# Feed-forward and recurrence stages in text order by the generator's clocks, and modulation products beside the down products

## The chip, the cores and the metric

One core of a Trainium2 chip runs the whole program. The metric is the device time of one execution in microseconds (us), the median over several runs. The engines are called as the profile calls them: PE (TensorE), DVE (VectorE), ACT (ScalarE), POOL (GpSimd) and SP (SyncE, which here only issues DMAs).

## The reference

The input is one sequence of 512 tokens of width 1024, all in fp32. Two layers of a modulated block are followed by two layers of a hybrid attention block and a last norm. The change touches the first two layers only. Cut to what matters, they are:

```python
for layer in range(2):
    mod = (silu(c) @ mod_w[layer] + mod_b[layer]).reshape(1, 3, 3, 1024)   # shift, scale, gate
    h, g = sublayer_input(x, norm_g[layer, 0], mod[:, 0])                  # rmsnorm, scale, shift
    x = x + 0.5 * g * swiglu(h, ffn_w_gu[layer, 0], ffn_w_down[layer, 0])
    h, g = sublayer_input(x, norm_g[layer, 1], mod[:, 1])
    y = stick_breaking_attention(h) if layer == 0 else rglru_block(h)
    x = x + g * y
    h, g = sublayer_input(x, norm_g[layer, 2], mod[:, 2])
    x = x + 0.5 * g * swiglu(h, ffn_w_gu[layer, 1], ffn_w_down[layer, 1])

def swiglu(h, w_gu, w_down):                 # w_gu 1024 x 5632, w_down 2816 x 1024
    g, u = split(h @ w_gu, 2)
    return (silu(g) * u) @ w_down

def rglru_block(h, ...):                     # width 1280, 10 blocks of 128
    gate, xb = split(h @ w_in, 2)
    xc = causal_conv(xb)                     # 4 taps
    r, i = sigmoid(xc @ w_r + b_r), sigmoid(xc @ w_i + b_i)
    a = exp(-8 * r * softplus(-lam))
    b = sqrt(-expm1(-16 * r * softplus(-lam))) * (i * xc)
    hs = scan(a, b)                          # hs[t] = a[t] * hs[t-1] + b[t]
    return (gelu(gate) * hs) @ w_out
```

## The kernel before, in words

The token axis is the free axis: `x` lies as eight tiles of 128 channels x 512 tokens. The stages run one after another: ffn00, stick (the attention layer), ffn01, ffn10, lru (the recurrence), ffn11, hybrid layers 0 and 1.

**Products.** An fp32 product is made of three PE matmuls of 512 columns in a reduced format: weight high part by input high part, weight high by input low, weight low by input high. So every operand needs two tiles: for weights `wh` (an ACT cast of the loaded chunk) and `wl` (chunk minus `wh`, on DVE or POOL), for inputs pairs like `hH, hL`, `gH, gL`, `xH, xL`, `yH, yL`, `aH, aL`.

**Stream.** All weights come from HBM in one list of entries (`segments`, L82, `layout`, L197). An entry is a `raw` tile of 128 x 1024 (512 KB), loaded by one DMA on SP's queue into a ring of 4 (`stream_dma`, L581). A weight entry holds 8 slots of 128 x 128, in two halves of 4. Between the weight entries stand 144 modulation entries: a `raw` tile multiplied by `cact` and summed on DVE in one custom instruction (`raw<-raw,cact`), eight of them to a vector such as (0, 2, 1) (layer 0, sublayer 2, scale). The numbers in `mod(0, 2, 1, 0.68, 0.78)` (L99) say between which fractions of its stage's weight stream the eight stand. `stream_step` (L606) converts the next entry; `ahead` keeps four halves converted in front of PE, in rings of five `wh` and five `wl` (L622).

**Normalization.** The first jobs of a stage start on unnormalized input: `begin` (L979) multiplies weights with `gH, gL` (x times its scale) while the column sums of squares (`o<-ones,sq`), the reciprocal root, its spreading by `o<-diag,ones`, and the normalized `ht`, `hH`, `hL` are made. What the shift adds is made apart: `wshift` sums weights times shift on DVE, `T<-ones,wshift` sums it over partitions on PE. At ffn00 that is `start` (L867). `FIRST` (L72) says how many blocks of 128 output columns a feed-forward stage starts in this way.

**Order of work.** One Python generator per little task issues the instructions. A virtual time `vt` goes on with each matmul; `spawn` queues a task, `pump` runs those that are due, and a task's `yield 0.7` comes back 0.7 us of `vt` later. In stick and the hybrid layers the program runs under `planned` (L380): the instructions of PE, DVE, ACT and POOL stand in the engine queues in the order in which the text issues them, each engine has a modelled clock (`clocked`, L390), and a bare `yield` comes back at the modelled end of what the task issued. In ffn00 to ffn11 and lru only the pieces in `begin` and `start` have a fixed order; the rest is ordered by the framework's scheduler.

**Recurrence** (`lru`, L1378). Jobs are `xb0` to `xb9` (then `conv` on DVE, giving `xH, xL`), `ri0` to `ri9` (two small products per block, then `gate_ri`), `ga0` to `ga9` (the gate half of `w_in`), and the output product `wo`. `beta` takes an ACT Sqrt of `om`, then on DVE a product and the scan `om<-ra,ix`. `out` is an ACT Gelu (`ge`) that frees the product's PSUM bank, a DVE product by the scan, and the split into `yH, yL`. There are eight PSUM banks: four `mm`, two `z`, one `T`, one `o`.

Of the kernel before, what the change touches and what calls it, by code (L numbers as in the profile page):

```python
# [71 lines left out]
FIRST = {(0, 0): 6, (0, 1): 4, (1, 0): 4, (1, 1): 4}  # L72
# [9 lines left out]
def segments():  # L82
# [4 lines left out]
    def ffn(l, i, mods):  # L87
# [3 lines left out]
        jobs += [(f"gu{j}", [gu[j]], KD) for j in range(n, 2 * KF)]  # L91
# [3 lines left out]
    def mod(l, s, j, a, b):  # L95
# [3 lines left out]
    ffn(0, 0, [mod(0, 0, 2, 0.16, 0.28), mod(0, 1, 1, 0.28, 0.40), mod(0, 1, 0, 0.40, 0.52), mod(0, 1, 2, 0.52, 0.64),  # L99
               mod(0, 2, 1, 0.68, 0.78), mod(0, 2, 0, 0.78, 0.88), mod(0, 2, 2, 0.88, 0.98)])  # L100
# [36 lines left out]
    jobs += [(f"wo{m}", [wo[m]], KR) for m in range(4, KD)]  # L137
    segs.append(("lru", jobs, []))
# [38 lines left out]
def first_slots(segs):  # L177
# [3 lines left out]
    for name, jobs, _ in segs:  # L181
        for job in jobs:
            for kt in rows_of(job):
                for j, (_, _, cols) in enumerate(job[1]):
# [4 lines left out]
                    slot += len(cols) // 128  # L189
    return out  # L190
# [6 lines left out]
def layout(segs):  # L197

    slots, chunk_span = [], []
    for name, jobs, mods in segs:  # L200
        a = len(slots)
        for job in jobs:
            for kt in rows_of(job):
# [22 lines left out]
    for c in range(len(slots) // 8):  # L226
        if c >= n:
            entries.append(("w", slots[8 * c:8 * c + 8]))
# [115 lines left out]
class Kern:  # L344

    NSLOT = 74

    RAW = 4
    AHEAD = 4

# [10 lines left out]
    def __init__(self, tc, io, upto=None):  # L361
        self.tc, self.nc, self.io = tc, Front(self, tc.nc), io

# [175 lines left out]
    def mm(self, out, lhsT, rhs, start, stop, cost=None):  # L539
# [8 lines left out]
        self.matmul_at(out, (lhsT, rhs), cost, start)  # L548
# [14 lines left out]
    def stream_init(self, entries):  # L563
# [6 lines left out]
        self.w_conv = 0  # L570
        self.n_w, self.kept = 0, []
# [5 lines left out]
        self.act_busy = False  # L577
# [3 lines left out]
    def stream_dma(self):  # L581
        nc = self.nc
        while self.e_dma < len(self.entries):
# [17 lines left out]
            else:  # L601
                break
            self.raws[self.e_dma] = raw
            self.e_dma += 1

    def stream_step(self):  # L606
# [3 lines left out]
        nc = self.nc  # L610
        if e[0] == "mod":
# [5 lines left out]
            if m == KD - 1 and vec != (0, 0, 1):  # L617
                self.mod_end(vec, 0, KD)
        else:
            j = self.w_conv % 2  # L620
            w = raw[j] if type(raw) is list else raw[:, 512 * j:512 * j + 512]
            h = self.wpool.tile([128, 512], F32R, name=self.name("wh"), tag="wh", bufs=self.AHEAD + 1)  # L622
            l = self.wpool.tile([128, 512], F32R, name=self.name("wl"), tag="wl", bufs=self.AHEAD + 1)
            if self.act_busy:
                nc.vector.tensor_copy(h, w)
            else:
                nc.scalar.copy(h, w)
            self.pool_credit += self.pool_low
# [17 lines left out]
        self.stream_dma()  # L646

# [40 lines left out]
    def take(self, n):  # L688
# [3 lines left out]
        self.slot += n  # L692
        h, l = self.parts[c]
# [61 lines left out]
    def mod_of(self, vec):  # L755
        assert (vec, KD - 1) in self.full, vec
# [98 lines left out]
    def h_high(self, kt, gs, shift, bc):  # L855
# [8 lines left out]
        self.h.append((h, l))  # L864
        return lambda: nc.vector.scalar_tensor_tensor(l, t, s, h.bitcast(F32), OP.add, OP.subtract)

    def start(self, tags):  # L867
# [33 lines left out]
        def factors():  # L901
# [27 lines left out]
            self.kept = []  # L929
# [1227 lines left out]
```

## Time and profile before

| | |
|---|---|
| median of 3 runs | 3085.96 us (3082.9 to 3088.1) |
| profiled execution, its own time | 3085.68 us |
| its span in the profile | 3084.0 us |
| mean granted TensorE clock | 0.987 |
| busy: PE, DVE, ACT, POOL | 97%, 62%, 43%, 35% of the span |
| stages: ffn00, stick, ffn01, ffn10 | 0 to 408, 408 to 683, 683 to 1042, 1042 to 1401 us |
| lru, ffn11, hybrid 0, hybrid 1 | 1401 to 1625, 1625 to 1992, 1992 to 2526, 2526 to 3084 us |

Busy is the time that instructions of an engine took, by their records. Matmul records overlap (each is longer than the distance to the next), so PE's busy share does not tell how fast it goes; the distance between starts does. A stage is bounded here by the first matmul of one stage and that of the next. Most helpers record every operation under one line (L328 for DVE, ACT and POOL, L547 for matmuls), so instructions are told apart by their tiles.

### The profile page before, as it was taken

How to read it: one execution, taken by the hardware profiler on the slowest of the kernel's cores; microseconds unless marked ns; L12 is line 12 of the kernel's file. 1: busy time of each engine (PE TensorE's matmuls, PEld its weight loads, DVE VectorE, ACT ScalarE, POOL GpSimd, SP SyncE). 2: the span in 40 equal slices, each digit the busy share in tenths (PEclk: the TensorE clock that was granted, in tenths of full speed). 3: DMA queues.
4: the chain of work that ended last, by engine and by line, in shares of the span. 5: the costliest groups of instructions: out<-in, count | busy, mean ns of one | idle time of the engine just before them, and what ended most of it. 6: DMA issues, size and time to landing. Idle time of an engine off the chain costs nothing. (4 is left out here: it accounts for less than half of the span.)

```text
span 3084.0 us, 39072 instructions
## 1 busy us (share of the span) xinstructions
PE 2977.1 (97%) x13752; PEld 2475.4 (80%) x13752; DVE 1902.0 (62%) x3409; ACT 1312.9 (43%) x2520; POOL 1085.0 (35%) x802
## 2 busy tenths in 40 slices
PE   7999999989999999999899999999999999999998
PEld 5788877768888888887688888888888878888886
DVE  7844476676444655568965333578676556867653
ACT  3333245544332333324734333356456534645652
POOL 4554754440001200013531001343443684334466
PEclk9999999999999999999999999999999999999999
DMA  6454554413333344462222223354343335434322
GB/s 241 158 198 175 194 160 113 119 64 137 137 137 133 120 171 152 156 211 82 81 94 92 96 97 115 110 166 122 103 123 110 109 117 157 123 110 124 110 85 93
DMA packets 132643, 400.53 MB, mean 130 GB/s; under 512 B 18528, under 2 KB 19040, under 8 KB 132448
## 3 DMA queue, kind: packets, MB, share of 16 engines
q1 hardware_dynamic: 132448, 398.04, 39.2%
q8 instruction: 109, 1.79, 0.2%
q14 instruction: 86, 0.70, 0.1%
HBM read 343.44 MB, written 6.30 MB: 113 GB/s over the span
## 5 line engine op out<-in xcount | busy, mean ns | idle before, releaser
L328 POOL TENSOR_TENSOR wl<-raw,wh 128x512 fp32r<-128x512 f32 x574 | 815.3, 1427 | 905.1 <-ACT wh L328 852.2
L328 ACT CAST wh<-raw 128x512 fp32r<-128x512 f32 x968 | 596.0, 620 | 1063.3 <-PE mm L547 926.9
L547 PE MATMUL mm<-hH,wh 128*128 128x512 f32 x1584 | 622.1, 393 | 13.6 <-ACT ge L328 9.8
L547 PE MATMUL mm<-hL,wh 128*128 128x512 f32 x1584 | 620.6, 392 | 2.6 <-DVE hL L328 2.6
L547 PE MATMUL mm<-hH,wl 128*128 128x512 f32 x1584 | 619.7, 391 | 0.0
L328 DVE TENSOR_TENSOR wl<-raw,wh 128x512 fp32r<-128x512 f32 x396 | 290.3, 735 | 363.4 <-ACT wh L328 360.7
L547 PE MATMUL mm<-gH,wh 128*128 128x512 f32 x1016 | 407.2, 401 | 6.2 <-DVE v L328 3.9
L547 PE MATMUL mm<-gH,wl 128*128 128x512 f32 x1016 | 398.5, 392 | 1.5 <-POOL wl L328 1.5
L547 PE MATMUL mm<-gL,wh 128*128 128x512 f32 x1016 | 397.8, 392 | 0.0
L547 PEld LDWEIGHTS mm<-hH,wh 128*128 128x128 f32 x1584 | 299.6, 189 | 77.4 <-ACT ge L328 10.2
L547 PEld LDWEIGHTS mm<-hL,wh 128*128 128x128 f32 x1584 | 299.7, 189 | 67.0 <-DVE hL L328 5.3
L547 PEld LDWEIGHTS mm<-hH,wl 128*128 128x128 f32 x1584 | 299.5, 189 | 62.5
L328 DVE CUSTOM_DVE_ANT_0 raw<-raw,cact 128x1024 f32<-128x1024 f32 x144 | 207.8, 1446 | 187.0 <-DMA raw<-ws 180.1
L547 PE MATMUL mm<-aH,wl 128*128 128x512 f32 x704 | 274.0, 389 | 0.0
L547 PE MATMUL mm<-aH,wh 128*128 128x512 f32 x704 | 273.9, 389 | 0.0
L328 POOL TENSOR_TENSOR sq<-x 128x512 f32<-128x512 f32 x7 | 7.6, 1086 | 730.7 <-DVE x L328 730.7
L547 PEld LDWEIGHTS mm<-gH,wl 128*128 128x128 f32 x1016 | 191.4, 188 | 44.7 <-POOL wl L328 2.7
L547 PEld LDWEIGHTS mm<-gH,wh 128*128 128x128 f32 x1016 | 192.1, 189 | 42.0 <-issue 4.3
L547 PEld LDWEIGHTS mm<-gL,wh 128*128 128x128 f32 x1016 | 192.1, 189 | 35.0
L547 PEld LDWEIGHTS mm<-aH,wl 128*128 128x128 f32 x704 | 132.1, 188 | 27.6 <-POOL wl L328 0.4
L547 PEld LDWEIGHTS mm<-aH,wh 128*128 128x128 f32 x704 | 132.1, 188 | 27.5
L547 PE MATMUL mm<-wide,wh 128*128 128x512 f32 x384 | 149.4, 389 | 0.0
(271 smaller groups left out, 4706.6 us busy)
## 6 DMA issues: line engine op xcount, KB each, us to landing
raw<-ws SPq DMA_DIRECT2D x629, 512.0 KB, 3.3
ks<-rH SPq DMA_DIRECT2D x80, 128.0 KB, 3.2
kl<-rL SPq DMA_DIRECT2D x80, 128.0 KB, 2.6
qs<-rH SPq DMA_DIRECT2D x56, 128.0 KB, 3.9
qs<-rL SPq DMA_DIRECT2D x56, 128.0 KB, 3.7
keep<-ws SPq DMA_DIRECT2D x16, 256.0 KB, 5.9
ks<-qkH SPq DMA_DIRECT2D x32, 128.0 KB, 3.5
kl<-qkL SPq DMA_DIRECT2D x32, 128.0 KB, 3.1
```

The costliest lines, as they stand in the source:

```text
L328: r = f(*args, **kw)
L547: self.nc.tensor.matmul(out, lhsT, rhs, start=start, stop=stop, skip_group_check=True)
```

## The change

It runs ffn01, ffn10, ffn11, lru, and what follows the start of ffn00, under `planned`; fixed waits in the tasks become bare `yield`. In these stages a new mode `free` converts each half chunk (`operand`) and each modulation product (`product_sum`) in a task of its own, and `either` puts each `wl` on POOL or DVE by their modelled clocks. `wh` and `wl` move from rings of five into the common arena (74 to 84 tiles). The modulation vectors of ffn00, ffn01 and ffn10 move to the down products, the last third of a stage, and two of ffn10's six move into ffn01. `FIRST` of ffn01 goes from 4 to 6 blocks. A wait of 6.0 us of `vt` is put ahead of the column sums in `start`, and `begin` waits for the modelled end of `sq`. The table `SEVEN` is empty for every stage, so the code that reads it issues nothing; it is left out below.

```diff
-FIRST = {(0, 0): 6, (0, 1): 4, (1, 0): 4, (1, 1): 4}
+FIRST = {(0, 0): 6, (0, 1): 6, (1, 0): 4, (1, 1): 4}
...
-    ffn(0, 0, [mod(0, 0, 2, 0.16, 0.28), mod(0, 1, 1, 0.28, 0.40), mod(0, 1, 0, 0.40, 0.52), mod(0, 1, 2, 0.52, 0.64),
-               mod(0, 2, 1, 0.68, 0.78), mod(0, 2, 0, 0.78, 0.88), mod(0, 2, 2, 0.88, 0.98)])
+    ffn(0, 0, [mod(0, 0, 2, 0.53, 0.60), mod(0, 1, 1, 0.60, 0.66), mod(0, 1, 0, 0.667, 0.73), mod(0, 1, 2, 0.73, 0.79),
+               mod(0, 2, 1, 0.79, 0.85), mod(0, 2, 0, 0.85, 0.91), mod(0, 2, 2, 0.91, 0.97)])
...
-    ffn(0, 1, [mod(1, 0, 1, 0.05, 0.35), mod(1, 0, 0, 0.35, 0.65), mod(1, 0, 2, 0.65, 0.95)])
-    ffn(1, 0, [mod(1, 1, 1, 0.02, 0.2), mod(1, 1, 0, 0.2, 0.4), mod(1, 1, 2, 0.4, 0.6),
-               mod(1, 2, 1, 0.68, 0.78), mod(1, 2, 0, 0.78, 0.88), mod(1, 2, 2, 0.88, 0.98)])
+    ffn(0, 1, [mod(1, 0, 1, 0.53, 0.65), mod(1, 0, 0, 0.667, 0.74), mod(1, 0, 2, 0.74, 0.81),
+               mod(1, 1, 1, 0.81, 0.88), mod(1, 1, 0, 0.88, 0.96)])
+    ffn(1, 0, [mod(1, 1, 2, 0.667, 0.74), mod(1, 2, 1, 0.74, 0.81), mod(1, 2, 0, 0.81, 0.88), mod(1, 2, 2, 0.88, 0.96)])
...
-    NSLOT = 74
+    NSLOT = 84
...
+    def either(self, out, a, b, op):
+
+        if self.free:
+            t = max(self.made.get(x.tensor.name, 0.0) for x in (a, b))
+            pool = max(self.clock["gpsimd"], t) + 1.29 < max(self.clock["vector"], t) + 0.68 + 0.7
...
+    def product_sum(self, vec, m, raw):
...
+        yield max(0.01, self.made[raw.tensor.name] - self.vt)
+        self.nc.vector.tensor_tensor_reduce(raw, raw, self.cact, 1.0, 0.0, OP.mult, OP.add, accum_out=out[:, m:m + 1])
+        del raw
+        self.in_ring -= 1
+        self.stream_dma()
...
+    def operand(self, i, raws, first):
...
+        self.shifts(w, 4 * i)
+        h = self.t("wh", dt=F32R)
+        self.nc.scalar.copy(h, w)
+        yield
+        l = self.t("wl", dt=F32R)
+        self.either(l, w, h.bitcast(F32), OP.subtract)
...
+            yield 6.0
             late.extend(self.shift_cols((0, 0), 8))
...
         def factors():
-            yield self.CHAIN[0] if (l, s) != (0, 2) else 7.0
+            if self.timed:
+                yield max(0.1, self.made[self.sq[0].tensor.name] - self.vt + 0.1)
...
-                yield 0.7
+                yield
                 nc.vector.tensor_tensor(a, sg, u, OP.mult)
...
+        with self.planned() if not self.timed else contextlib.nullcontext():
+            self.free = True
+            self.ffn_rest(l, i, n, act, low, evac)
+            self.free = False
...
-            yield 3.8
+            yield
             h = self.t("xH", dt=F32R)
...
-        self.pool_low = 1.0
+        self.free = True
         for n in range(4):
             self.spawn(conv(n, ps[n], late[n], tags[n]))
...
-                self.act_busy = n == 2
...
+                with self.planned() if l or i else contextlib.nullcontext():
+                    self.ffn(l, i)
...
+                    with self.planned():
+                        self.lru()
```

In the pieces below a row is one instruction, or several alike (x3), with its line, its operation, its output and inputs (the number behind a name tells tiles apart) and its shape.

DVE behind the start of ffn00, before: `wshift` sums weights times shift, `ISA raw,mod<-raw,cact` is a modulation product, `a` and `wide` belong to the first blocks' activations.

```order
L328 TENSOR_SCALAR wshift_699<-keep_326,mod_365 128x128
L328 ISA raw_740,mod_738<-raw_740,cact 128x1024
L328 ISA mod_738 128x1
L328 SCALAR_TENSOR_TENSOR wshift_699<-keep_326,mod_365,wshift_699 128x128
L328 TENSOR_TENSOR a_835<-sg_834,mm_787 128x512
...
L328 TENSOR_TENSOR wide_83<-a_835,aH_866 128x512
L328 SCALAR_TENSOR_TENSOR wshift_699<-keep_373,mod_365,wshift_699 128x128
L328 ISA raw_789,mod_738<-raw_789,cact 128x1024
L328 ISA mod_738 128x1
L328 SCALAR_TENSOR_TENSOR wshift_699<-keep_373,mod_365,wshift_699 128x128
```

DVE at the same place with the change:

```order
L346 TENSOR_SCALAR wshift_678<-keep_326,mod_365 128x128
L346 SCALAR_TENSOR_TENSOR wshift_678<-keep_326,mod_365,wshift_678 128x128 x3
L346 SCALAR_TENSOR_TENSOR wshift_678<-keep_327,mod_365,wshift_678 128x128 x4
L346 TENSOR_SCALAR wshift_678<-keep_372,mod_365 128x128
L346 SCALAR_TENSOR_TENSOR wshift_678<-keep_372,mod_365,wshift_678 128x128 x3
L346 SCALAR_TENSOR_TENSOR wshift_678<-keep_373,mod_365,wshift_678 128x128 x4
L346 TENSOR_TENSOR a_842<-sg_841,mm_794 128x512
L346 TENSOR_TENSOR wide_83<-a_842,aH_856 128x512
```

The modulation products are gone from among the `wshift` instructions; one pair of `a` and `wide` now stands behind the last of them.

PE at the start of ffn01, before: `mm<-oH/oL` are the last of the attention's output product, `z, mm<-gH/gL` the first of ffn01, `o<-ones,sq` the column sums.

```order
L547 MATMUL mm_5753<-oH_5579,wh_5646 128x512
L547 MATMUL mm_5753<-oL_5581,wh_5646 128x512
L547 MATMUL mm_5753<-oH_5579,wl_5647 128x512
L547 MATMUL z_5788<-gH_5589,wh_5673 128x512
...
L547 MATMUL mm_5790<-gH_5641,wl_5729 128x512
L547 MATMUL o_5842<-ones,sq_5587 128x1 x4
L547 MATMUL mm_5791<-gH_5641,wh_5728 128x512
```

PE at the same place with the change:

```order
L568 MATMUL mm_5760<-oH_5588,wh_5632 128x512
L568 MATMUL mm_5760<-oL_5590,wh_5632 128x512
L568 MATMUL mm_5760<-oH_5588,wl_5654 128x512
L568 MATMUL z_5790<-gH_5598,wh_5684 128x512
...
L568 MATMUL mm_5792<-gH_5598,wl_5718 128x512
L568 MATMUL o_5819<-ones,sq_5596 128x1 x4
L568 MATMUL mm_5793<-gH_5598,wh_5684 128x512
```

The sums stand 33 matmuls behind the last output product before, and 9 behind it now.

ACT in the recurrence, before: `om<-om` is the last Sqrt, `ge` a Gelu that frees a PSUM bank, `yH` the cast behind the product with the scan, `wh` a weight cast.

```order
L328 ACTIVATE om_12158<-om_12158 128x512
L328 ACT_TABLE_LOAD
L328 ACTIVATE ge_12193<-T_12029 128x512
L328 ACTIVATE ge_12195<-o_12116 128x512
L328 CAST wh_12245<-raw_11997 128x512
...
L328 CAST wh_12329<-raw_12121 128x512
L328 CAST yH_12218<-ge_12193 128x512
L328 CAST yH_12220<-ge_12195 128x512
L328 CAST wh_12350<-raw_12202 128x512
L328 ACTIVATE ge_12242<-mm_12197 128x512
L328 CAST yH_12264<-ge_12242 128x512
```

ACT at the same place with the change:

```order
L346 ACTIVATE om_12176<-om_12176 128x512
L346 ACT_TABLE_LOAD
L346 ACTIVATE ge_12227<-T_12063 128x512
L346 ACTIVATE ge_12229<-o_12154 128x512
...
L346 ACTIVATE ge_12268<-mm_12231 128x512
...
L346 ACTIVATE ge_12306<-mm_12270 128x512
L346 CAST wh_12328<-raw_12132 128x512
L346 CAST wh_12330<-raw_12132 128x512
L346 CAST yH_12341<-ge_12227 128x512
L346 CAST yH_12346<-ge_12229 128x512
L346 ACTIVATE ge_12350<-mm_12308 128x512
```

The third, fourth and fifth Gelu stood behind the casts `yH` of the first two blocks; two of them now stand ahead of these casts, the third behind.

## Rows read from the trace of the kernel before

**Rows 1.** The page: busy time, share of the span and instructions of each engine.

```profile
PE 2977.1 (97%) x13752; PEld 2475.4 (80%) x13752; DVE 1902.0 (62%) x3409; ACT 1312.9 (43%) x2520; POOL 1085.0 (35%) x802
```

**Rows 2.** Two stages: length; busy us (count) of PE, PEld, DVE, ACT, POOL; clock, DMA share, GB/s.

```profile
1042.00:1401.00 359.00, 358.83 (x1595) 297.30 (x1595) 209.68 (x332) 117.78 (x194) 30.13 (x21) 1.00 0.48 167
1401.00:1625.00 224.00, 205.19 (x886) 167.06 (x885) 176.53 (x219) 115.36 (x183) 101.89 (x71) 0.95 0.24 83
```

**Rows 3.** Timeline of PE: ffn00's sums and two matmuls behind them; two matmuls of ffn01.

```profile
112.13 0.59 PE L547 MATMUL T<-ones,wshift 128*128 128x1 f32 x2 [5.32 <-DVE wshift L328]
113.58 0.63 PE L547 MATMUL mm<-hH,wl 128*128 128x512 f32 x1
114.00 0.63 PE L547 MATMUL mm<-hH,wh 128*128 128x512 f32 x1
...
676.43 0.39 PE L547 MATMUL z<-gH,wh 128*128 128x512 f32 x1
676.66 0.39 PE L547 MATMUL z<-gL,wh 128*128 128x512 f32 x1
```

**Rows 4.** Waits of PE, 0 to 2000 us: us in total, times, longest us.

```profile
PE mm L547 <- ACT ge L328: 9.8, 1, 9.8
PE T L547 <- DVE wshift L328: 5.3, 1, 5.3
PE o L547 <- DVE sq L328: 5.3, 2, 4.8
PE z L547 <- DVE xL L328: 4.9, 1, 4.9
PE o L547 <- POOL wl L328: 2.3, 1, 2.3
PE mm L547 <- DVE hL L328: 1.7, 3, 0.7
```

**Rows 5.** Short stretches behind two of the waits, columns as in rows 2.

```profile
108.00:118.00 10.00, 5.87 (x16) 4.81 (x17) 7.75 (x20) 2.28 (x5) 3.71 (x2) 0.50 0.54 177
1531.00:1542.00 11.00, 6.15 (x15) 4.86 (x16) 8.90 (x12) 5.51 (x10) 2.55 (x2) 0.53 0.11 43
```

**Rows 6.** Timeline of DVE, 72 to 120 us.

```profile
73.20 1.45 DVE L328 CUSTOM_DVE_ANT_0 raw<-raw,cact 128x1024 f32<-128x1024 f32 x1 [1.03 <-DMA raw<-ws]
...
79.59 1.78 DVE L328 SCALAR_TENSOR_TENSOR hL<-ht,mod,hH 128x512 fp32r<-128x512 f32 x1
...
87.08 0.74 DVE L328 SCALAR_TENSOR_TENSOR hL<-ht,mod,hH 128x512 fp32r<-128x512 f32 x1
...
106.16 1.21 DVE L328 CUSTOM_DVE_ANT_0 raw<-raw,cact 128x1024 f32<-128x1024 f32 x1
...
114.27 0.34 DVE L328 SCALAR_TENSOR_TENSOR wshift<-keep,mod,wshift 128x128 f32<-128x128 f32 x1
```

**Rows 7.** Timeline of ACT, then DVE, in the recurrence.

```profile
1532.45 0.62 ACT L328 CAST yH<-ge 128x512 fp32r<-128x512 f32 x1 [11.32 <-DVE ge L328]
...
1532.34 1.21 DVE L328 TENSOR_TENSOR_SCAN om<-ra,ix 128x512 f32<-128x512 f32 x1
```

**Rows 8.** Timeline of DVE at the end of the attention layer.

```profile
686.26 1.75 DVE L328 TENSOR_TENSOR sq<-sq,sqt 128x512 f32<-128x512 f32 x1
```

**Rows 9.** Stretches with the densest transfers, columns as in rows 2.

```profile
5.00:25.00 20.00, 12.79 (x48) 10.01 (x48) 12.78 (x29) 11.11 (x18) 6.14 (x4) 1.00 1.04 397
280.00:400.00 120.00, 120.00 (x530) 99.06 (x529) 56.06 (x68) 31.39 (x54) 81.38 (x56) 1.00 0.54 193
```

**Rows 10.** The page: a group (count, busy us, mean ns) and the DMA of raw (landing us).

```profile
L328 POOL TENSOR_TENSOR wl<-raw,wh 128x512 fp32r<-128x512 f32 x574 | 815.3, 1427 | 905.1 <-ACT wh L328 852.2
...
raw<-ws SPq DMA_DIRECT2D x629, 512.0 KB, 3.3
```

**Rows 11.** Timeline of POOL, 72 to 92 us.

```profile
77.32 3.50 POOL L328 TENSOR_TENSOR wl<-raw,wh 128x512 fp32r<-128x512 f32 x2 [3.76 <-ACT wh L328]
```

More of the change, by code (lines that the diff above doesn't have):

```diff
@@ L602, in stream_dma @@
                 break
+            for r in raw if type(raw) is list else (raw,):
+                self.made[r.tensor.name] = self.vt + 5.0
             self.raws[self.e_dma] = raw
@@ L610, in stream_step @@
         nc = self.nc
+        if e[0] == "mod" and self.free:
+            self.spawn(self.product_sum(e[1], e[2], raw))
+            del self.raws[self.e_conv]
+            self.e_conv += 1
+            return
         if e[0] == "mod":
@@ new lines, in operand @@
+    def operand(self, i, raws, first):
+        for r in self.reads.setdefault(i, raws):
+            yield max(0.01, self.made[r.tensor.name] - self.vt)
+        w = yield from first()
+        self.shifts(w, 4 * i)
+        h = self.t("wh", dt=F32R)
+        self.nc.scalar.copy(h, w)
+        yield
+        l = self.t("wl", dt=F32R)
+        self.either(l, w, h.bitcast(F32), OP.subtract)
+        self.parts[i] = (h, l)
+        del w, first
+        for r in raws:
+            self.left_raw[r.tensor.name] -= 1
+            if not self.left_raw[r.tensor.name]:
+                self.in_ring -= 1
+                self.stream_dma()
+        self.reads.pop(i)
@@ L692, in take @@
         self.slot += n
+        if c not in self.parts:
+            self.need(lambda: c in self.parts)
         h, l = self.parts[c]
@@ L755, in mod_of @@
     def mod_of(self, vec):
-        assert (vec, KD - 1) in self.full, vec
+        self.need(lambda: all((vec, k) in self.full for k in range(KD)))
         return self.mods[vec]
@@ new lines, in seven, with B, T, product @@
+    def seven(self, f, tt, act, low, last):
+        nc = self.nc
+        def B(k, o):
+            return lambda i: tuple(x[:, o:o + 256] for x in self.h[i + k])
+        def T(k):
+            return lambda i: tuple(x[:, 256 * (i % 2):256 * (i % 2) + 256] for x in tt[k - 1, i // 2])
+        def product(bank, mov, first=True):
+            for i in range(4):
+                xh, xl = mov(i)
+                wh, wl = self.take(1)
+                for n, (w, x) in enumerate(((wh, xh), (wh, xl), (wl, xh))):
+                    self.mm(bank, w, x, first and i == n == 0, i == 3 and n == 2, again=i == n == 0)
+                self.pump()
+        for _ in range(4):
+            self.job(f"q{f}")
+        b1 = self.bank("mm")[:, 0:256]
+        product(b1, B(0, 0))
+        base = self.t("base", 256)
+        nc.scalar.copy(base, b1)
+        b2 = self.bank("z")[:, 0:256]
+        product(b2, T(2))
+        u2 = self.t("u2", 256)
+        nc.vector.tensor_tensor(u2, base, b2, OP.add)
+        self.rel("z")
+        if self.behind:
+            self.behind()
+        b3 = self.bank("z")[:, 0:256]
+        product(b3, T(1))
+        u4 = self.t("u4", 256)
+        nc.vector.tensor_tensor(u4, u2, b3, OP.add)
+        self.rel("z")
+        product(b1, B(4, 0), False)
+        g = self.t("sg")
+        nc.scalar.activation(g[:, 0:256], b1, AF.Silu)
+        self.rel("mm")
+        b7 = self.bank("mm")[:, 0:256]
+        product(b7, T(3))
+        up = self.t("a")
+        nc.vector.tensor_tensor(up[:, 256:512], u4, b7, OP.add)
+        b3 = self.bank("mm")[:, 0:256]
+        product(b3, B(4, 256))
+        nc.vector.tensor_tensor(u4, u4, b3, OP.add)
+        self.rel("mm")
+        def right():
+            yield
+            nc.scalar.activation(g[:, 256:512], u4, AF.Silu)
+        self.spawn(right(), 0.1)
+        def behind():
+            self.behind = None
+            product(b7, T(4), False)
+            nc.vector.tensor_tensor(up[:, 0:256], u2, b7, OP.add)
+            self.rel("mm")
+            self.spawn(rest())
+        def rest():
+            yield 0.1
+            yield
+            nc.vector.tensor_tensor(up, g, up, OP.mult)
+            yield
+            h = self.t("aH", dt=F32R)
+            nc.scalar.copy(h, up)
+            yield
+            lo = low[f] if f < 12 else self.t("aL", dt=F32R)
+            self.either(lo, up, h.bitcast(F32), OP.subtract)
+            act[f] = (h, lo)
+        if last:
+            behind()
+        else:
+            self.behind = behind
```

273 lines of the change are left out of this document (208 added, 65 removed).

## The prediction

> **What bounds the kernel now.** I read the page first: PE is busy 97% of the span [rows 1], so only what stops or slows PE can move the time. Then the stages: ffn10 takes 359 us for 66 weight entries of 24 matmuls, 1584 in all [rows 2], that is 0.227 us from start to start, the distance that two neighbours in ffn01 show too [rows 3]. That stage has nothing to give. The recurrence takes 224 us with PE busy in 205 [rows 2]. The waits of PE say where the idle time up to 2000 us lies [rows 4]: 9.8 us in front of one product of the recurrence, 5.3 in front of ffn00's column sums of `wshift`, 5.3 before sums of squares (4.8 of it at the start of ffn01), 4.9 and 2.3 in the recurrence, 1.7 in three pieces behind `hL`. A wait costs more than itself: after the one that ends at 112.13 us the next matmuls start 0.42 us apart instead of 0.23 [rows 3], with a granted clock of 0.50 against 1.00 in ffn10, and around the end of the 9.8 us the clock is 0.53 [rows 2, 5]. So each matmul in such a stretch loses 0.195 us.
>
> **The change, term by term.** The sum is made against the profiled execution, 3085.68 us (span 3084.0 and 1.7 around it), which lies 0.3 below the median.
>
> *Start of ffn00.* PE stands from 106.8 to 112.1 us, and DVE's last `wshift` starts at 114.27 us and ends about 0.3 later [rows 6]. In front of it in DVE's queue stand four modulation products that now move to the down products: one that waited 1.03 us for its DMA and ran 1.45, and three of 1.21 [rows 6] (two of the three are not shown), together 6.1 us; one pair of `a` and `wide`, two instructions of 0.6 us, moves behind it. So `wshift` would end at 114.6 - 6.1 - 1.2 = 107.3. PE comes to the last of the sums six matmuls (1.4 us) later in its own order, but without the 1.7 us behind `hL`, which two of these products had delayed: 106.8 + 1.4 - 1.7 = 106.5, or up to 3 us later where a block now in text order waits for its `hL`. At most the whole place goes: 5.3 idle, 14 matmuls at 0.195 = 2.7, and 1.7, together 9.7. At least 4.5 goes, where 2.5 us of wait stay and with them the slow stretch. I take 7.5, nearer to the upper end, because `wshift` comes out within 1 us of PE.
>
> *The recurrence.* PE's 9.8 us are a wait for a PSUM bank, which the third block's Gelu frees. That Gelu stood on ACT behind `yH` of the first block, and `yH` waited 11.32 us for a DVE product [rows 7] that stands in DVE's queue between the last scans; the last one starts at 1532.34 [rows 7]. With the change the third and fourth Gelu stand ahead of `yH`, so the bank is free before PE asks for it; the fifth, behind two `yH`, has until two further products of 24 matmuls (10.9 us) are through. That removes 9.8 and the slow stretch behind it (13 matmuls, 2.6). The wait of 2.3 for a `wl` on POOL came with a slow stretch too (8 matmuls, 1.5, an estimate by the same 0.195): `operand` makes those tiles in order of need, so 3.8 goes as well. The wait of 4.9 for `xL` stays: four blocks of convolution stand in DVE's queue ahead of it, before and after. In return the small products `ri` now stand in pairs with no other matmul between; I put half a microsecond on each of four, an estimate between 0 and the 1.2 of two ACT instructions. Net: 16.2 - 2 = 14, with 5 and 16 as ends.
>
> *Start of ffn01.* Here the change makes PE ask earlier: the sums of squares stand 9 matmuls behind the last output product instead of 33. They wait for the last `sq`, which ends at 688.0 [rows 8]. The first matmuls of ffn01 ran at 676 us [rows 3], 12 us earlier, so it is the chain DVE, ACT, DVE behind each tile of x that sets this end, and not PE. The new queue has two `wl` and some `wshift` work less in front of it; I put its end 2.5 us earlier. But 24 matmuls (5.4 us) that PE did while it waited now come after it: 5.4 - 2.5 = 2.9 slower. The ends are -1 (`sq` 6 us earlier) and +5 (not earlier at all).
>
> *Starts of ffn10, the recurrence and ffn11.* Sums come after 12 matmuls instead of 15; 3 x 0.227 = 0.7 either way for each, 2 in all, taken as nothing.
>
> *Down products.* Forty modulation entries in 0.30 of 66 weight entries are two to each in ffn00, 32 in 0.29 are 1.7 in ffn01 and ffn10, against about one before. PE takes 5.44 us for an entry, so three loads of 512 KB in that time are 289 GB/s. Down products ran with 193, and 5 to 25 us shows 397 [rows 9], so the rate is there. The ring of four gives a load 4/3 x 5.44 = 7.25 us from issue to the end of its use. Landing takes 3.3 [rows 10]; then come the product, 1.2 [rows 6], or an ACT cast of 0.62 [rows 7] and `wl`, 1.43 [rows 10]. I take nothing; what covers it is the ring and the four converted halves ahead of PE (10.9 us), and the price without them is in the first rival.
>
> *`wl`.* Some 220 subtractions go from DVE to POOL, at 1.43 us each [rows 10]. POOL is busy for 30 of 359 us in ffn10 [rows 2], and PE there never waited: nothing. What this does to DVE is seen at 77 to 89 us: one `hL` took 1.78 us while POOL had `wl` from 77.32 to 80.82, another 0.74 at 87.08 with POOL idle [rows 6, 11]. So up to 1.04 us more on a product counts in the first rival. The Trainium skill, page SBUF — State Buffer, section SBUF: two separate sides, has a rule that speaks against the move: DVE and GpSimd share one port pair, an exclusive lock, so that the loser fully blocks. The trace agrees, with 1.04 us on this instruction. By the rule each moved `wl` could block one DVE instruction, 229 us in all, in stages where DVE has about 150 us each to spare, so the sum would be the same.
>
> The hybrid layers and the middle of the attention layer keep their order; SP issues as many DMAs as before. Sum: -7.5 - 14 + 2.9 = -18.6, so 3085.7 - 18.6 = **3067**.
>
> **The rivals.**
>
> *The ring runs short (slower).* If a load stays r us in the ring, an entry with two products takes 3/4 r. Four loads under way at 397 GB/s land in 5.3 us; with a product of 1.2 + 1.04 r is 7.5, an entry 5.7 us, and the 59 such entries lose 15 us, which the 10.9 us ahead in each of three stages swallow. It decides from r = 8.4 (an entry of 6.31): 59 x 0.87 less 33 is 18.6, all that is gained. At r = 9 it is 77 - 33 = 44, and 44 - 19 = 25 slower, 3111. Against it: landing 3.3. Chance 0.09.
>
> *The recurrence waits elsewhere.* In ACT's new order the `wh` of the eighth block's second half stands behind five `yH`. If the scans end no earlier than at 1533 us [rows 7], those five casts go on to about 1540 while PE wants this `wh` at about 1530: 10 of the 14 us come back, 3077. It decides from scans that end after 1524 or so. For it: DVE has the same ten convolutions and scans to do. Against it: all ten Sqrt now stand together on ACT, and PE's earlier wait for `wl` had held up what feeds them. Chance 0.20.
>
> *Text order costs what it gains.* The feed-forward stages had no wait; now each `wl`, activation and product stands where a modelled clock puts it (1.29 us for a POOL `wl` that takes 1.43 [rows 10]), and a late one holds all behind it. One wait of 0.1 us for each of 198 entries is 20 us: 3087, no change; the same rival stands for queues that come out much as the scheduler had them. Chance 0.14.
>
> *More goes.* The waits for `xL` and at ffn01 go too (4.9 + 2.1 and 4.8 + 1.3, and the 2.9 is not paid), and both places above go whole: 3067 - 16 - 4 = 3047. Chance 0.07.
>
> **How the numbers follow.** The forecast has 0.50, with 3058 to 3076 from its own bounds. A measurement of this kernel can tell about 0.2%, 6.2 us, from no change: faster is below 3079.8. Faster takes the forecast 0.50, most of the second rival 0.17, the last 0.07 and a little of the third 0.02: 0.76. Same takes 0.03 of the second and 0.09 of the third: 0.12. Slower takes the first rival 0.09 and 0.03 of the third: 0.12. The range goes from 3052 to 3087: left out are the first rival, most of the last and the upper end of the third.
>
> **What would show it.** Right: no wait of PE for `wshift` over 2.5 us and a granted clock of 1.00 at 108 to 118 us; no wait for `ge`, and the recurrence about 14 us shorter; a wait for `sq` at ffn01 of about 8 us instead of 4.8; ffn10 still 359 us. Wrong: waits for `wl` or `wh` in the down products with loads that land in over 5 us (first rival); a wait for `wh` of the gate half of the recurrence (second); ffn10 or ffn11 longer by several us in many small pieces (third).

## The result and the profile after

The changed kernel takes 3122.51 us (median of 4 runs, 3116.8 to 3126.62) against 3087.03 for the kernel before in the same runs (4 runs, 3082.9 to 3095.11). The ratio is 1.0110, with an interval of 1.0083 to 1.0137. It is slower by about 35 us; the forecast was 3067, 20 faster.

The page of the changed kernel, its span and the engines' busy time, the second to set beside [rows 1]:

```profile
span 3122.8 us, 39254 instructions
...
PE 2994.8 (96%) x13756; PEld 2483.8 (80%) x13756; DVE 1923.3 (62%) x3200; ACT 1257.4 (40%) x2516; POOL 1376.6 (44%) x1023
```

PE has 18 us more of busy time for the same matmuls (its mean granted clock is 0.983, before 0.987), and the rest is waiting. POOL has 292 us more, DVE hardly more. The two stretches that answer to [rows 2], shifted by where the stages begin now; columns as there:

```profile
1068.40:1427.40 359.00, 358.10 (x1591) 296.47 (x1591) 175.89 (x209) 109.50 (x195) 152.39 (x108) 1.00 0.41 142
1427.40:1645.30 217.90, 201.28 (x871) 163.41 (x870) 184.84 (x211) 105.28 (x178) 107.64 (x75) 0.97 0.27 87
```

The first reads like before (359 us, clock 1.00), only with `wl` moved (POOL 152 us instead of 30). The second, around the recurrence, is 217.9 us instead of 224. So neither of the two is what was lost. The waits of PE up to 2012 us, against [rows 4] (in total, times, longest):

```profile
PE o L568 <- DVE sq L346: 10.9, 2, 9.0
PE mm L568 <- ACT wh L346: 8.5, 6, 2.6
PE o L568 <- DVE diag L346: 8.4, 4, 6.4
...
PE z L568 <- DVE xL L346: 6.5, 1, 6.5
PE z L568 <- ACT tr L346: 6.1, 3, 2.4
PE mm L568 <- POOL wl L346: 4.8, 7, 1.0
PE mm L568 <- DVE hL L346: 4.6, 4, 1.7
...
PE T L568 <- DVE wshift L346: 0.8, 1, 0.8
```

The waits for `ge` and for `wshift` at 107 us are gone, and the one for POOL's `wl` in the recurrence is 1.0 instead of 2.3. New are waits for `tr`, for `wh` in the down products and more for `hL`, and the one for `sq` is 9.0 instead of 4.8. Each row is small; the sum is found by stages. The table gives their lengths in us, from the first matmul of a stage on its unnormalized input to that of the next, both read from PE's timeline; "down" are the down products of a feed-forward stage, and "blocks" all that comes before them in it.

| | before | changed | difference |
|---|---|---|---|
| ffn00 blocks / down | 272.9 / 120.0 | 271.6 / 130.3 | -1.3 / +10.3 |
| stick | 270.9 | 276.8 | +5.9 |
| ffn01 blocks / down | 250.7 / 119.7 | 259.2 / 122.5 | +8.5 / +2.8 |
| ffn10 | 362.3 | 363.2 | +0.9 |
| recurrence | 206.4 | 200.2 | -6.2 |
| ffn11 | 363.1 | 365.6 | +2.5 |
| hybrid 0 / hybrid 1 | 546.2 / 550.9 | 558.5 / 554.2 | +12.3 / +3.3 |

They sum to +39, the difference of the two spans (3122.8 - 3084.0). Down products at full pace take 119.7. What one profile can tell: `a_sums33` below has the changed kernel's instructions in the same order on all engines and the queue of SP, and its stages differ from these by up to 1.9 us, hybrid 0 by 3.9. `a_nopad`, in the same order up to ffn10, differs by 3.8 in stick and 3.1 in ffn01's blocks, and `b_lru` and `b_pad`, with the order of before in ffn00, have 123.1 and 124.6 for its down products. So a stage in one profile is known to some 4 us.

The losses lie in four places: ffn00's down products, the start of ffn01, the hybrid layers, and less clearly stick. The sum had only the second, with 2.9 us.

### The profile page after: what moved, and what is told of

Same layout as the page of the kernel before. It is cut to its first block, busy times and chain, and to the rows that moved or that the text cites. A ratio compares the mean times of both kernels' runs of the same rounds, so it can differ in the third digit from the quotient of the medians.

```text
span 3122.8 us, 39254 instructions
## 1 busy us (share of the span) xinstructions
PE 2994.8 (96%) x13756; PEld 2483.8 (80%) x13756; DVE 1923.3 (62%) x3200; ACT 1257.4 (40%) x2516; POOL 1376.6 (44%) x1023
## 4 chain that ended last, share of the span: by engine, by line
PE 63%; DVE 10%; ACT 1%; DMA 1%; issue 1%; POOL 1%; SPq 0%; DVEq 0%; POOLq 0%; ACTq 0%
PE mm L568 56%; PE z L568 3%; PE o L568 2%; PE T L572 1%; DVE xc L346 1%; DVE sw L346 1%; DVE om L346 1%; DMA raw<-ws 1%; DVE wl L346 1%; DVE x L346 1%; DVE ix L346 1%; DVE wshift L346 0%; DVE hL L346 0%; PE T L568 0%; POOL wl L346 0%
## 5 line engine op out<-in xcount | busy, mean ns | idle before, releaser
L346 POOL TENSOR_TENSOR wl<-raw,wh 128x512 fp32r<-128x512 f32 x795 | 1118.1, 1418 | 1468.8 <-ACT wh L346 1198.2
L346 ACT CAST wh<-raw 128x512 fp32r<-128x512 f32 x970 | 561.0, 616 | 266.3 <-DMA raw<-ws 258.0
L568 PE MATMUL mm<-gH,wh 128*128 128x512 f32 x1032 | 417.4, 404 | 6.5 <-DVE v L346 4.1
L568 PE MATMUL mm<-gH,wl 128*128 128x512 f32 x1032 | 407.7, 395 | 1.5 <-POOL wl L346 1.5
L568 PE MATMUL mm<-gL,wh 128*128 128x512 f32 x1032 | 407.7, 395 | 0.0
L346 DVE TENSOR_TENSOR a<-sg,mm 128x512 f32<-128x512 f32 x77 | 52.9, 687 | 460.9 <-PE mm L568 457.2
L346 DVE TENSOR_TENSOR wl<-raw,wh 128x512 fp32r<-128x512 f32 x175 | 243.2, 1400 | 76.6 <-ACT wh L346 76.6
L346 DVE CUSTOM_DVE_ANT_0 raw<-raw,cact 128x1024 f32<-128x1024 f32 x144 | 233.1, 1644 | 20.5 <-DMA raw<-ws 11.6
L346 ACT CAST aH<-a 128x512 fp32r<-128x512 f32 x88 | 54.1, 620 | 331.4 <-DVE a L346 331.4
```

The source lines that it names most:

```text
L346: r = f(*args, **kw)
L568: self.nc.tensor.matmul(out, lhsT, rhs, start=start, stop=stop, skip_group_check=True)
```

## The experiments

Fourteen kernels were run in four groups on three chips, up to ten times each, and each group with the kernel before on the same chip. The medians of before in these groups went from 3086.0 to 3093.2, so ratios are compared.

| kernel | median | before | ratio, interval |
|---|---|---|---|
| a_mods_back | 3109.03 | 3089.28 | 1.0061, 1.0041 to 1.0080 |
| a_rings2 | 3136.29 | 3089.28 | 1.0149, 1.0133 to 1.0165 |
| b_arena | 3140.47 | 3089.28 | 1.0161, 1.0146 to 1.0176 |
| b_mods | 3105.91 | 3089.28 | 1.0048, 1.0031 to 1.0065 |
| b_pad | 3098.14 | 3093.00 | 1.0022, 1.0010 to 1.0034 |
| a_nopad | 3108.49 | 3093.00 | 1.0050, 1.0030 to 1.0070 |
| a_sums33 | 3127.44 | 3093.00 | 1.0114, 1.0092 to 1.0137 |
| b_lru | 3092.13 | 3093.00 | 1.0003, 0.9993 to 1.0013 |
| a_first4 | 3116.56 | 3085.99 | 1.0094, 1.0079 to 1.0109 |
| a_sums33_slots | 3114.58 | 3085.99 | 1.0091, 1.0076 to 1.0107 |
| a_wl_dve | 3106.06 | 3085.99 | 1.0058, 1.0043 to 1.0073 |
| a_raw6 | 3107.77 | 3085.99 | 1.0068, 1.0051 to 1.0085 |
| a_three | 3083.82 | 3093.22 | 0.9972, 0.9962 to 0.9983 |
| a_three_ri | 3082.51 | 3093.22 | 0.9971, 0.9960 to 0.9982 |

### The down products of ffn00

In the changed kernel at 351 us, DVE, then POOL, ACT and PE, each from its timeline:

```profile
351.14 2.31 DVE L346 CUSTOM_DVE_ANT_0 raw<-raw,cact 128x1024 f32<-128x1024 f32 x1
...
353.38 2.29 DVE L346 CUSTOM_DVE_ANT_0 raw<-raw,cact 128x1024 f32<-128x1024 f32 x1
...
355.60 2.31 DVE L346 CUSTOM_DVE_ANT_0 raw<-raw,cact 128x1024 f32<-128x1024 f32 x1
```

```profile
352.33 4.50 POOL L346 TENSOR_TENSOR wl<-raw,wh 128x512 fp32r<-128x512 f32 x2
```

```profile
361.88 1.14 ACT L346 CAST wh<-raw 128x512 fp32r<-128x512 f32 x2 [10.48 <-DMA raw<-ws]
```

```profile
362.55 0.50 PE L568 MATMUL mm<-aH,wh 128*128 128x512 f32 x1 [2.61 <-ACT wh L346]
...
382.58 0.80 PE L568 MATMUL mm<-aH,wh 128*128 128x512 f32 x1 [2.48 <-ACT wh L346]
```

Three modulation products follow one another on DVE, 2.3 us each instead of 1.21 [rows 6], while POOL makes two `wl` in 4.50 us. SP issues no load from 349.0 us until these two `wl` are done at 356.8: they read the `raw` tile whose slot SP needs next. SP's waits from 340 to 366 us:

```profile
SPq L617 <- POOL wl L346: 12.7, 3, 6.8
SPq L617 <- DVE mod L346: 4.0, 4, 3.2
```

So the next weights land late, ACT's cast waits 10.48 us for its load and PE 2.61 for the cast. PE waits like this twice in this stretch, the second time with a slower clock behind it (a mean of 0.66 from 380 to 390 us).

POOL's part is not new in this stage. All `wl` on POOL and all products from 280 to 410 us, before and then with the change (count; shortest, median and longest in ns):

```profile
L328 POOL TENSOR_TENSOR wl<-raw,wh x48: 1281/1299/2323, 280.2 to 409.2; 128x512 fp32r<-128x512 f32 x48
L328 DVE CUSTOM_DVE_ANT_0 raw<-raw,cact x22: 1225/1330/2293, 283.2 to 387.8; 128x1024 f32<-128x1024 f32 x22
```

```profile
L346 DVE CUSTOM_DVE_ANT_0 raw<-raw,cact x37: 1210/1224/2311, 283.7 to 397.3; 128x1024 f32<-128x1024 f32 x37
L346 POOL TENSOR_TENSOR wl<-raw,wh x30: 1269/1372/2326, 282.9 to 409.6; 128x512 fp32r<-128x512 f32 x30
```

Before, POOL made every `wl` of this stage; now it makes 30 of 44 in this stretch and DVE 14. New are the products: 37 instead of 22. And the order of before was near its limit: where its own profile has no wait in these down products, `b_lru` and `b_pad` waited 2.7 and 4.1 us there for `wl` and `wh`. Against these two the loss is 6 to 7 us instead of 10.3.

**a_mods_back** puts the products back:

```diff
-    ffn(0, 0, [mod(0, 0, 2, 0.53, 0.60), mod(0, 1, 1, 0.60, 0.66), ...
+    ffn(0, 0, [mod(0, 0, 2, 0.16, 0.28), mod(0, 1, 1, 0.28, 0.40), ...
```

> The changed kernel with the modulation products at their places of before (the two mod tables of before, all else as changed). Theory 1, the products beside the down products starve the weight ring: the waits of PE for wh and wl at 354 to 382 us and around 1026 and 1044 us go with their slow clock, about 10 us in ffn00 and 3 in ffn01, so 3122 becomes about 3109; the column sums of wshift in ffn00 may wait again (up to 5). Rival, text order itself makes these waits: they stay and the time is 3122.

ffn00's down products take 119.7 us again, ffn01's too, with no wait for `wh` or `wl` in them. The ratio falls by 0.0049 (15 us). The rival falls: text order alone makes no such wait. Its products in the same stretch:

```profile
L346 DVE CUSTOM_DVE_ANT_0 raw<-raw,cact x23: 1210/2298/2332, 285.8 to 386.2; 128x1024 f32<-128x1024 f32 x23
```

Half of them took 2.3 us and nothing was lost, so long products alone are not the cause.

**b_mods**, the kernel before with the two tables of the change:

> The kernel before with only the two mod tables of the change. Theory 1 in its strict form (four slots, two products per weight entry): waits for wh and wl in the down products of ffn00 as in the change, 3087 becomes about 3097, less 5 to 10 where the sums of wshift at 107 us no longer wait. Theory 1 with the port as a part of it (products of 2.3 us instead of 1.2 because POOL has half of the wl): in ffn01 and ffn10 wl is on DVE here, so no waits there, and only ffn00 can lose; then 3080 to 3087.

ffn00 down 136.5, ffn01 122.8, ffn10 124.5 instead of 119.7 to 120.0; the sums of `wshift` at 107 us still wait, 1.75 us. The strict form comes nearer: the scheduler's order starves as well, and even in ffn01 and ffn10, where `wl` is on DVE. Denser products cost 16.5, 3.1 and 4.8 us in these stages with no `wl` moved.

**a_wl_dve** keeps the products where they are and takes POOL away from them:

```diff
-            pool = max(self.clock["gpsimd"], t) + 1.29 < max(self.clock["vector"], t) + 0.68 + 0.7
+            pool = not self.on_dve and max(self.clock["gpsimd"], t) + 1.29 < max(self.clock["vector"], t) + 0.68 + 0.7
```

with `on_dve` set in `ffn_rest`.

> The changed kernel with every wl of the feed-forward stages' rest on DVE, none on POOL. If the products starve the ring because POOL's wl doubles them (2.3 us instead of 1.2): the products take about 1.2 again, the waits for wh and wl at 354 to 382 us go, ffn00 falls by up to 10 us and the total to about 3112. If four slots and three loads per entry are too few by themselves: the waits stay, 3122, or more, since DVE then has products and wl in one queue.

A stretch of 35 us of ffn00's down products in the changed kernel, then one in this kernel; columns as in [rows 2]:

```profile
350.00:385.00 35.00, 28.75 (x118) 21.93 (x117) 24.75 (x27) 6.69 (x12) 18.34 (x12) 0.96 0.62 224
```

```profile
340.00:375.00 35.00, 35.00 (x156) 29.01 (x155) 27.53 (x42) 8.76 (x15) 6.13 (x6) 1.00 0.76 271
```

PE is busy all the time at full clock, and the loads go faster (271 GB/s instead of 224). DVE's timeline there, two `wl` and two products in a row:

```profile
344.61 1.28 DVE L346 TENSOR_TENSOR wl<-raw,wh 128x512 fp32r<-128x512 f32 x2
345.82 1.22 DVE L346 CUSTOM_DVE_ANT_0 raw<-raw,cact 128x1024 f32<-128x1024 f32 x1
...
347.03 1.23 DVE L346 CUSTOM_DVE_ANT_0 raw<-raw,cact 128x1024 f32<-128x1024 f32 x1
```

Products take 1.2 us, and all `wl` beside them cost DVE 0.6 each. ffn00's blocks gain 4 us too; the ratio falls by 0.0052. In ffn00 this does more than undo the change, since before every `wl` there was on POOL.

**a_raw6** leaves both and gives the ring two slots more (`RAW = 6`, `NSLOT = 80`):

> The changed kernel with six raw slots instead of four (arena 80 tiles instead of 84). If the ring's length is what the denser products lack: the waits for wh and wl in the down products of ffn00 and ffn01 go, 10 and 2 us, and SP's queue in the hybrid layers waits less for ring slots, so some of their 16 us as well: 3098 to 3112. If landing or DVE is the limit and not the slots: waits stay, 3122; if the four tiles fewer in the arena matter, the feed-forward stages show new waits.

ffn00 down 121.9, ffn01 119.7: the slots too are enough. The hybrid layers hardly change (554.2 and 556.9). So in the changed order ffn00's loss takes three things together: two products to a weight entry, `wl` on POOL beside them, and a ring of four. Taking any one of them away removes it, or nearly.

### The start of ffn01

The changed kernel, PE's wait and the last `sq` on DVE:

```profile
702.08 1.84 PE L568 MATMUL o<-ones,sq 128*128 128x1 f32 x8 [8.98 <-DVE sq L346]
```

```profile
701.24 0.69 DVE L346 TENSOR_TENSOR sq<-sq,sqt 128x512 f32<-128x512 f32 x1
```

Stage ffn01 began at 690.0, so `sq` ends 11.9 us into it; before it was 12.2 (675.8 to 688.0). The chain is no earlier, and PE stands 9.0 us in front of it instead of 4.8.

**a_sums33** wanted the sums 7.0 us of modelled time later:

> The changed kernel with one wait of before: the sums of squares at the start of ffn01 are issued 7.0 us of modelled time later, as before, instead of at the modelled end of sq. If the place of the sums is what costs there: the wait of 9.0 us for sq shrinks by about 5 (24 matmuls), and the column sums that follow may wait less; 3122 becomes about 3116. If DVE's chain alone sets the time (six blocks of wshift instead of four): the wait moves by no more than 1 or 2 us, 3120 to 3122.

It moved nothing: by the generator's clock 7.0 us are over after the same 9 matmuls, since its modelled PE waits for modelled inputs. The order is the changed kernel's, and so is the ratio (1.0114 and 1.0110).

**a_sums33_slots** counts matmuls instead:

```diff
-            if self.timed:
+            if (l, s) == (0, 2):
+                slot = self.slot
+                yield 0.1
+                while self.slot - slot < 11:
+                    yield 0.05
+            elif self.timed:
```

> The changed kernel with the sums of squares of ffn01 held back until 33 matmuls of the stage are issued, six blocks kept. If the place of the sums alone costs: the wait shrinks by 24 x 0.227 = 5.4, from 9.0 to about 3.6, and 3122 becomes about 3117. If sq is later too because of the wshift work of six blocks, the wait shrinks just as much but sq still ends some 13 us behind the last output product, and the stage gains less than 5.

ffn01's blocks fall from 259.2 to 252.4 (252.6 and 252.5 in the two versions built on it below; 255.8 to 260.2 in all with six blocks and the sums unmoved). No wait for `sq` is left; in its place stands one for PSUM banks, which the last tiles of x still hold when six blocks ask for six of them (waits of PE there):

```profile
PE mm L568 <- DVE x L346: 5.9, 2, 4.2
```

**a_first4**, `FIRST` of ffn01 at 4 as before:

> The changed kernel with four blocks instead of six on unnormalized input at the start of ffn01. In the order of this kernel the sums of squares come to stand 30 matmuls behind the last output product instead of 9, and four blocks need half of the wshift work on DVE. If the six blocks are what ffn01 loses by: the wait for sq falls from 9.0 to about 5 us, the wait for wshift with its slow clock goes, ffn01 from 381 to about 372 us, in all 3122 to 3113. If DVE's late chain does it whatever the blocks: 381 stays.

Its sums stand 30 matmuls behind, the wait is 4.87, and ffn01's blocks take 255.1: the earlier place of the sums came with the six blocks. Most of the 8.5 us is the place.

### The hybrid layers

PE, DVE and POOL have there the order of before. SP does not: it is not under `planned`, and the pad, four empty slots, shifts the weight entries by half an entry, so that one more `raw` stands ahead of many groups of `qs`, `ks`, `kl` loads.

**b_pad**, the pad alone in the kernel before:

```diff
     jobs += [(f"wo{m}", [wo[m]], KR) for m in range(4, KD)]
+    jobs.append(("pad", [], 4))
```

> The kernel before with the pad alone: four empty slots behind the recurrence. From there on the halves of the weight entries fall half an entry later in the jobs, and in SP's queue one load of raw comes to stand ahead of many groups of qs, ks, kl loads of the hybrid layers. Theory 3, these loads then wait behind a raw whose ring slot is not free: hybrid layer 0 gets longer by some 10 us and layer 1 by some 3, so 3087 becomes about 3100. Rival, the hybrid layers lose time through the arena or through how they are entered: 3087, both hybrid layers as before.

**a_nopad**, the changed kernel without it:

> The changed kernel without the pad. Theory 3: both hybrid layers come back to 546 and 551 us (from 558.5 and 554), about 3106. Rival, arena: they stay, 3120.

`a_nopad` has 546.3 and 548.7 us in the hybrid layers, as before; the ratio falls by 0.0060 (18 us). Of the versions with `wh` and `wl` in the arena and a ring of four, the six with the pad have 1110 to 1117 us in both layers together and the three without it 1095 to 1098. In `b_pad` the pad costs less (550.6 and 552.4, together 1103.0, against 1097.1 in the kernel before and 1100.0 in `b_lru`, which has the order of before there). One place in hybrid 0, changed kernel, SP's timeline (DMA issues), and PE's:

```profile
2263.55 19.74 SPq L617 DMA_DIRECT2D raw<-ws  x4
2283.38 0.47 SPq L1412 DMA_DIRECT2D qs<-rH  x1
...
2285.91 2.62 SPq L1412 DMA_DIRECT2D ks<-rH  x4
```

```profile
2290.53 0.30 PE L568 MATMUL z<-ks,qs 128*128 128x128 f32 x1 [1.04 <-DMA ks<-rH]
2292.06 0.30 PE L568 MATMUL z<-kl,qs 128*128 128x128 f32 x1 [1.24 <-DMA kl<-rL]
```

The same group in `a_nopad`:

```profile
2254.93 11.29 SPq L616 DMA_DIRECT2D raw<-ws  x3
2266.32 1.15 SPq L1411 DMA_DIRECT2D qs<-rH  x1
...
2269.55 2.46 SPq L1411 DMA_DIRECT2D ks<-rH  x4
```

```profile
2276.78 0.22 PE L567 MATMUL z<-ks,qs 128*128 128x128 f32 x1
```

With the pad four `raw` issues stand ahead, and they take until 2283.3, waiting for ring slots; `ks` is issued at 2285.91 and PE waits for it at 2290.53. Without, it is three, and PE finds `ks` there, 7 us after its issue.

**b_arena** and **a_rings2** were to test another cause, the move of `wh` and `wl` out of their rings of five:

```diff
-            h = self.wpool.tile([128, 512], F32R, name=self.name("wh"), tag="wh", bufs=self.AHEAD + 1)
+            h = self.t("wh", dt=F32R)
```

> The kernel before with wh and wl in the common arena (84 tiles) instead of the rings of five, nothing else. Theory 2: the attention layer and the hybrid layers become longer by 15 to 22 us, 3102 to 3109. Rival (the rings do nothing): 3087, or a little faster where ACT no longer waits for PE.

> The changed kernel with wh and wl back in rings of five in the attention layer, the hybrid layers and the starts of stages (arena of 74 tiles as before); the free stages keep their wh and wl in the arena. Theory 2, the rings held ACT and the loads back to PE's pace, and without them the loads of ks, qs and the casts on ACT collide: the attention layer gets back about 7 us and the hybrid layers 15, so about 3100. Rival, the two layers lose time because their waits of one to two microseconds fall differently, not because of the rings: 3122 and the same waits.

Neither shows what it was made for. `b_arena` has hybrid layers of 549.8 and 549.6, close to before, and loses 51 us elsewhere: ffn00 down 139.4, its blocks 280.4, the recurrence 218.7. There the scheduler orders, and it orders worse without the rings. `a_rings2`, with rings and pad, has 552.3 and 552.1, as `b_pad`; its feed-forward stages lose (ffn00 down 134.1, ffn11's blocks 253.5 instead of 246.0), perhaps by the smaller arena. By all these the pad costs 3 to 6 us in the kernel before, with rings, and 12 to 22 in the changed kernel without. Why the arena makes it dearer was not tried apart.

### The recurrence

**b_lru** is the kernel before with the recurrence alone under `planned`, rings kept:

> The kernel before with the recurrence alone in text order (its new waits, wl on POOL, wh on ACT, rings of five kept). If the recurrence gains what the change shows there: its excess over full pace falls from 27 to about 19 us, 3087 becomes about 3079, with waits for tr between the ri products and none for ge. If text order gains only together with the arena (rings of five hold ACT behind PE): waits for wh or ge stay and the time is 3085 to 3095.

206.4 becomes 202.1, but ffn11 takes 367.6 instead of 363.1: its sums now wait 2.34 us for `sq`. Nothing is left of it in the time. In the changed kernel, ACT, two rows:

```profile
1541.78 0.61 ACT L346 ACTIVATE ge<-mm 128x512 f32<-128x512 f32 x1
...
1559.26 1.17 ACT L346 CAST yH<-ge 128x512 fp32r<-128x512 f32 x2 [13.25 <-DVE ge L346]
```

`yH` still waits 13.25 us for DVE's `ge`, but the Gelu of the third block ran 17 us before it, and no product waits for its bank. The gain was taken elsewhere. ACT and PE where the small products stand in pairs:

```profile
1511.76 0.68 ACT L346 ACTIVATE tr<-z,lru 128x512 f32<-128x512 f32 x1
1512.34 0.68 ACT L346 ACTIVATE ti<-z,lru 128x512 f32<-128x512 f32 x1
1512.91 0.81 ACT L346 ACTIVATE ra<-tr,lru 128x512 f32<-128x512 f32 x1
1513.62 0.80 ACT L346 ACTIVATE tu<-tr,lru 128x512 f32<-128x512 f32 x1
1514.33 1.12 ACT L346 CAST wh<-raw 128x512 fp32r<-128x512 f32 x2
1515.36 0.68 ACT L346 ACTIVATE tr<-z,lru 128x512 f32<-128x512 f32 x1
```

```profile
1512.50 0.50 PE L568 MATMUL z<-xH,wh 128*128 128x512 f32 x1 [2.36 <-ACT tr L346]
...
1516.09 0.50 PE L568 MATMUL z<-xH,wh 128*128 128x512 f32 x1 [1.93 <-ACT tr L346]
...
1526.31 0.50 PE L568 MATMUL z<-xH,wh 128*128 128x512 f32 x1 [1.76 <-ACT tr L346]
```

Three ACT instructions of one block and two `wh` stand between the `tr` that frees a bank for the first product of a pair and the `tr` that frees it for the second (1511.76 and 1515.36). PE waits for a `tr` three times, about 2 us each.

**a_three_ri** gives the second product of a pair two `mm` banks:

```diff
-            self.rel("z", 2)
+            self.rel("mm" if n in (3, 5, 7, 9) else "z", 2)
...
-                r, i = self.proj(name, lambda kt: xs[n], ("z", "z"))
+                r, i = self.proj(name, lambda kt: xs[n], 2 * ("mm" if n in (3, 5, 7, 9) else "z",))
```

It stands on **a_three**, the changed kernel with the pad gone, `wl` as in `a_wl_dve` and the sums as in `a_sums33_slots`.

> The changed kernel with three edits together: no pad, every wl of the feed-forward stages' rest on DVE, the sums of squares of ffn01 behind 33 matmuls. If the three losses lie in different places and add up: 3122 less 14, 16 and 8 is about 3084 on the scale of the first runs, 3 below the kernel before, and the profile's stages would sum to some 14 us less than before (ffn00 387, ffn01 about 368, hybrid layers 546 and 549). If one hides another (wl on DVE makes sq later, or the pad's cost comes only with late loads): 3095 to 3105.

> The three edits, and the second small product of each pair ri2 ri3, ri4 ri5, ri6 ri7, ri8 ri9 on banks mm instead of z. If the waits for tr of about 2 us each are waits for the two z banks of the product just before: they go, the recurrence falls by 4 to 6 us (from 200 to about 195). If ACT is what is late: the waits move to the next product on these banks or to wl, and the recurrence stays at 198 to 200.

`a_three`: the ratio is 0.9972. From 1.0110 the three single edits took 0.0060, 0.0052 and 0.0019, together 0.0131, which leaves 0.9979. So, within the intervals, they are separate causes and they add up. ffn00 takes 387.6, ffn01 372.3, the hybrid layers 548.6 and 548.9; stick, 275.4, keeps its loss. This version is faster than both kernels. In `a_three_ri` the waits for `tr` are gone, of the waits of PE in this stretch these remain as the longest:

```profile
PE z L567 <- DVE xL L345: 6.5, 1, 6.5
PE mm L567 <- DVE xL L345: 2.3, 1, 2.3
PE o L567 <- DVE sq L345: 1.9, 1, 1.9
```

The recurrence falls from 200.3 to 196.8 (198.2 to 200.4 in the versions with this order and no rings). The price moved in part: 2.3 of the 6.4 us now wait for `xL`. In the whole time the two versions cannot be told apart (0.9971 and 0.9972).

## Why the prediction was wrong

Two steps that it put at nothing cost most, the down products (13.1 us) and the order in SP's queue (15.6). Three others were mis-sized.

*Start of ffn00, -7.5 forecast, -1.3 measured.* PE waits for no `wshift`, as forecast, and 92 to 118 us runs at a clock of 1.00. But this came by luck: the last `wshift` ended at 111.3 us, not at 107.3, and PE came to the sums at 112.8, not at 106.5. The step that failed is PE's way there. It forecast that the 1.7 us behind `hL` would go; they became 4.6, and the wait for `diag` ahead of them, which the sum did not have, went from 4.7 to 6.4 (3.6 to 5.4 in the other versions, so part of it is chance). PE had the gaps and the half clock earlier, instead of behind `wshift`. What makes these `hL` late was not settled; with `wl` off POOL they still take 2.4. The blocks of ffn00 then take 267.4 to 267.9 us (three versions), against 270.8 to 272.2 in all others of the changed order; but POOL had `wl` there before as well, so this need not be what the term missed.

*The recurrence, -14 forecast, -6.2 measured, of which ffn11 gives back 2.5.* The mechanism was right: `ge` no longer stops PE, and POOL's `wl` only for 1.0 us. Mis-sized was the term for the pairs of `ri`, 2 us: PE waits 6.1 there, and taking these waits away shortened the stage by 3.5. `xL`, taken as unchanged, went from 4.9 to 6.5. What ffn11 gives back, a wait of 2.0 for `sq`, was "taken as nothing". The wait for `wh` of the second rival came with 0.7 us instead of 10.

*Start of ffn01, +2.9 forecast, +8.5 measured.* The place of the sums was right. The step "I put its end 2.5 us earlier" failed: `sq` ended 11.9 us into the stage against 12.2. That makes 5.4 - 0.3 = 5.1 by the prediction's own sum; undoing the place gave 6.8. The remaining 1.7 were not taken apart; they are less than one profile differs from the next, and a new wait of 0.8 for `wshift` with half clock behind it stands there too.

*Down products, 0 forecast, +13.1 measured (10.3 and 2.8).* The step that failed reads "I take nothing". It gave a weight entry 3.3 us to land, 0.62 for the cast and 1.43 for one `wl`. In ffn00's down products a load took 4.8 us to land (median, 3.3 before), and the slot comes free only behind both `wl` of the entry, 4.50 us at 352; SP waited 6.8 for them. The product, taken at 1.2, was given 2.25 only in the first rival, at 0.09, as if POOL's `wl` came with the change there. But of the 220 `wl` that it moved to POOL none is ffn00's, and [rows 9] had POOL busy for 81 of 120 us in these very down products. There the rival was the case: with two products to an entry in place of one, the ring had no room left. Its sign, loads that land in over 5 us, did not come. The rule of the Trainium skill (page SBUF — State Buffer, section SBUF: two separate sides) that DVE and GpSimd lock each other out of a shared port was named there. The trace agrees with it once more, 2.31 against 1.22 us for one instruction. The prediction set its price to nothing because DVE had time to spare; what ran short was slots of the ring, and taking `wl` off POOL took the loss away.

*Hybrid layers and stick, 0 forecast, +15.6 and +5.9 measured.* The step that failed reads "SP issues as many DMAs as before". It counted and did not look at their order, though SP is the one queue that no clock of the generator holds. `a_nopad` shows the pad, which changes that order, as the cause in the hybrid layers. Of stick's 5.9 the cause stays open: kernels with the changed kernel's order there had 272.7 to 279.5, those with the order of before 270.6 to 272.4, and `b_arena` 274.7.

The text-order rival was right only in that order matters: ffn10, with everything under `planned`, took 363.2 instead of 362.3.

## What to carry to other kernels

When loads get denser, add up how long each holds its slot of a short ring, with the times that its readers take in that very stage beside their neighbours on other engines. Look at the order in every queue, the one that only issues DMAs too; a shift of half an entry in a weight stream can put a load that waits for its slot ahead of a load that PE needs. And a generator's clock decides only what it models: holding an instruction back by a count of matmuls moved it, holding it back by modelled time did not.

## What was not expected

All `wl` of a feed-forward stage fit on DVE beside two products per weight entry: at 0.6 us each two of them take less of DVE than POOL's two added to two products (1.3 against 2.2 us), and loads reached 271 GB/s. A kernel agrees with itself less well than 0.2% from one group of runs, or chip, to the next: the kernel before had medians of 3086.0, 3087.0, 3089.3, 3093.0 and 3093.2 us.
